# Unnormalised first input products, later S5 parameters and reordered output operands in a two-branch decoder layer

## The chip, the core and the metric

The kernel runs on one core of a Trainium2 chip. Its time is the device time of one execution in microseconds (us); the time before is the median of three runs. A profile records one execution: TensorE's matmuls (PE) and its weight loads (PEld), VectorE (DVE), ScalarE (ACT), GpSimd (POOL), the DMA queues, and SyncE (SP), which issues most of the DMAs. The span of a profile runs from the first to the last recorded instruction.

## What is computed

The reference is one decoder layer with two parallel branches, for 1024 tokens of width 1024 in float32. What matters here is its beginning and its end:

```
h = rms_norm(x, g_pre)                 # x * g_pre / sqrt(mean(x*x) + eps), per token
proj = h @ w_in                        # 512 + 512 + 1280 + 1280 + 1024 + 1024 columns
s5_x, s5_g, lru_x, lru_g, gate_s, gate_l = split(proj)
y_s = s5_ssm(s5_x, ...)                # discretised complex state-space model, 32 groups
z_s = (GLU of gelu(y_s)) * silu(s5_g) @ w_bs
z_l = rg_lru(conv(lru_x)) * silu(lru_g) @ w_bl
merged = sigmoid(gate_s) * z_s + sigmoid(gate_l) * z_l
x = x + rms_norm(merged @ w_out, g_post)
x = x + (p @ w_ple) * sigmoid(x @ w_ple_gate)
```

The factor 1/sqrt(mean(x*x)+eps) belongs to a token, so it can be applied to `h` or to a column of `h @ w_in`; `g_pre` belongs to a row of `w_in`.

## The kernel before

Everything is kept transposed: 128 features on the partitions and 1024 tokens along a row, in two halves of 512. Every large product is split in three: each operand is cut into a rounded part (`hi`, made by ACT) and the rest (`lo = src - hi`, made by DVE or POOL), and `three` (L306 to L310) adds hi*hi, hi*lo and lo*hi in PSUM, so a block of 128x128 weights against 512 tokens is three matmuls. I call twelve such matmuls (two blocks against both halves, or one block pair) a **group**. The weights come in chunks through `Weights`: a DMA from SP, `hi` by ACT (L215), `lo` by DVE (L227), in a ring of six buffers of four blocks; `ahead` prepares a few buffers before TensorE needs them. The instructions of PE, DVE, ACT and POOL stand in the order in which the program writes them, each engine executes its own in that order, and the background generators in `bg` are advanced one step at each `tick`, that is about once a group. So the order of work around the change is fixed by where a step is written or at which tick it is taken.

The stages that the change touches:

- **w_ple.** Eight groups multiply `p` by `w_ple` (m = 0 to 7, tiles `ps_ple`); ACT copies each result to `ple_sb` (L710) and SP stores it. Meanwhile x arrives, ACT squares its eight columns `xt(k)` (L683), DVE adds the squares (L685), and DVE does the first 60 or so small steps of `s5_params`, the parameters of the state-space model (`prep_exp`).
- **The token factor.** `tok_rstd` (L377 on): 16 sums over partitions on PE (`pst_pre`), a short chain on DVE with one square root on ACT, eight diagonal tiles, and eight products that spread the factor over all partitions (`psb_pre`).
- **Two pairs of w_in columns**, u0 with u1 and then u2 with u3 (function `two`, tiles `ps_u`, eight groups each: one group for each column k of x). Before group k of the first pair `h_build` normalises (L729, DVE, the factor read from PSUM), rounds (L730, ACT) and takes the rest (L739, first half DVE, second half POOL). The second pair finds all of `h` ready. ACT takes the results out of PSUM (L748) in the order that the scan needs, and they are stored to DRAM. The rest of `s5_params` stands after the last `h_build` and in the ticks of the second pair; its powers and the input matrix `bb` are made by POOL (L604 to L661).
- **Light rows.** Eighteen products of `h` with one further column of w_in, four groups each (`light`, tiles `ps_L`), each followed by a sigmoid on ACT (L925). In their ticks runs the state-space model (`s5_all`): a table (`s5_table`), output weights on POOL (`s5_out_weights`), and for each of eight head blocks `s5_main`, whose weights `ta` DVE makes from `pw` and `bb` (L827 to L829) and PE transposes (`pwin`, L844).
- **w_out**, late in the kernel, is a block algorithm with sums of operands: `product` is one group, and its operands are B11, B21, T2, T3, T1, B22 and T4, each split in `op_split`. The order of the products is four of B11, two of B21, and then four times T2, T3, T1, B22 (tiles `oY`, `oZ`, `oW`, `oV`); the sums of weights `wS` for them come from POOL (L187) just in time. The operands T1 and B22 are split by the generator `out_ops` in the ticks behind B11.

Of the kernel before, what the change touches and what calls it, by code (L numbers as in the profile page):

```python
# [9 lines left out]
F32 = mybir.dt.float32  # L10
F32R = mybir.dt.float32r
I32 = mybir.dt.int32
AF = mybir.ActivationFunctionType
# [4 lines left out]
P = 128  # L18
# [110 lines left out]
class Weights:  # L129
# [116 lines left out]
def tile_hybrid_trunk(  # L246
# [21 lines left out]
    def page(i, name, dt=F32R):  # L268
        return page_pool[i].tile([P, 2 * NT], dt, tag=f"pg{i}", name=name)
# [36 lines left out]
    def three(ps, wb, xb, start, stop, more=False):  # L306
        (wh, wl), (xh, xl) = wb, xb
        T.matmul(ps, wh, xh, start=start, stop=False, skip_group_check=more)  # L308
        T.matmul(ps, wh, xl, start=False, stop=False, skip_group_check=more)  # L309
        T.matmul(ps, wl, xh, start=False, stop=stop, skip_group_check=more)  # L310
# [14 lines left out]
    def drain():  # L325
        while bg:
            tick()
# [116 lines left out]
    def quarter(t):  # L444
        return t.rearrange("p (k n) -> p k n", n=HT)
# [19 lines left out]
    sqs = [two_rows(i, f"sqs{i}") for i in (0, 1)]  # L465
    ple_sb = [two_rows(i, f"ple_sb{i}") for i in (4, 5, 13, 2)]
    scratch = page(8, "scratch", F32)
    NPAR = sum(n for _, n in SPAR)
    NPT = NPAR - 2048
# [15 lines left out]
    G.memset(toep, 0.0)  # L485
    G.memset(sgn, 1.0)
    G.memset(sgn[64:], -1.0)

    def load_x(ks):
        for k in ks:  # L490
# [170 lines left out]
        G.tensor_tensor(bb_2, bb_2, bt, ALU.add)  # L661

    prep = s5_params()
    seen = []

    def prep_steps(n):
        for _ in range(n):
            next(prep, None)

    def prep_exp(n):  # L670
        for _ in range(n):
            if not seen:
                seen.extend(["exp"] * (next(prep) == "exp"))

    def prep_until(mark):
        while next(prep, mark) != mark:
            pass

    prep_exp(24)

    def square(k):
        sq = sqs[k % 2][:, k // 2 % 2] if k else ssq
        S.activation(sq, xt(k), AF.Square)  # L683
        if 0 < k < ND - 1:
            V.tensor_tensor(ssq, ssq, sq, ALU.add)  # L685
            prep_exp(5)
# [5 lines left out]
    squares = {0: (0,), 1: (1, 2), 2: (3,), 3: (4,), 4: (5, 6), 5: (7,)}  # L692
    for m in range(ND):
        if m % 2 == 0:
            wb = W.next()
        if m == 7:
            prep_exp(100)
            next(stats)
        ps = wide(f"ps_ple{m}")
        for k in range(2):  # L700
            for h in range(2):
                three(ps[:, HALF[h]], wb[2 * (m % 2) + k], (p_hi[:, k, HALF[h]], p_lo[:, k, HALF[h]]), k == 0, k == 1)
        for k in squares.get(m, ()):
            sq = square(k)
            if k == ND - 1:
                ssqs.append(sq)
        if m == 7:
            next(stats)
        sb = ple_sb[m // 2][:, m % 2]
# [6 lines left out]
    for _ in stats:  # L716
        pass

    hq = {n: [quarter(page(i0 + j, f"h{n}{j}")) for j in range(2)]
          for n, i0 in (("B11", 0), ("B21", 4), ("B12", 10), ("B22", 12))}  # L720

    def hplain(k, h):
        hi, lo = hq[f"B{1 + k // 4}{1 + h}"]
        return hi[:, k % 4, :], lo[:, k % 4, :]

    def h_hi(k):
        for h in range(2):
            xs = xt(k, HALF[h])
            V.scalar_tensor_tensor(xs, xs, gpre[:, k:k + 1], rb[h], ALU.mult, ALU.mult)  # L729
            S.activation(hplain(k, h)[0], xs, AF.Copy)  # L730

    def h_build(k):
        if k == 0:
            h_hi(0)
        elif 0 < k < ND - 1:
            h_hi(k + 1)
        for h in range(2):
            hi, lo = hplain(k, h)
            (G if h else V).tensor_tensor(lo, xt(k, HALF[h]), hi.bitcast(F32), ALU.subtract)  # L739
        if k <= 0:  # L740
            h_hi(k + 1)
        if k == ND - 1:
            prep_until("den")

    def u_out(m, ps, tile):
        for h in range(2):
            up = tile(h).rearrange("p (j k) -> p j k", j=8)
            S.activation(up.rearrange("p j k -> p k j"), ps[h].rearrange("p (k j) -> p k j", j=8), AF.Copy)  # L748
# [3 lines left out]
    ups = quarter(page(9, "ups", F32))  # L752
# [3 lines left out]
    for t, ps in enumerate(two(ND, hplain, "u0", h_build, pair_of("u0"))):  # L756
        u_out(t, ps, lambda h: ups[:, 2 * t + h, :])

    def prep_rest():
        for _ in range(2):  # L760
            yield
            prep_steps(2)
        yield
        for _ in prep:
            pass

    bg.append(prep_rest())
    u2, u3 = two(ND, hplain, "u2", ps=pair_of("u2"))
    u_out(2, u2, lambda h: pro.tile([P, HT], F32, tag=f"up{h}", name=f"up{h}"))
    drain()  # L770
    pctx.close()

    ev = s5x.enter_context(tc.tile_pool(name="ev", bufs=2))
# [440 lines left out]
    def x1(k, h):  # L1214
        return x1p[k // 2][:, k % 2, HALF[h]]

    def out_ops():
        for name, i, q in (("T1", 16, 11), ("B22", 7, 22)):
            op(name, i)
            for k in range(4):  # L1220
                op_split(name, k, mg(q, k), k % 2 == 1)
                if k % 2:
                    flush()
                    yield

    def last_op():
        op("T4", 12)
# [35 lines left out]
    def product(ps, name, start):  # L1263
# [3 lines left out]
            three(ps, wb, (hi[:, k, :], lo[:, k, :]), start and k == 0, k == 3, not start)  # L1267
        tick()

    xs = [bank(f"oX{p}") for p in range(4)]  # L1270
    for p_ in range(4):
        product(xs[p_], "B11", True)
        S.activation(mixt(2 * p_, 1), xs[p_], AF.Copy)
        if p_ > 1:
            S.activation(mixt(2 * p_, 0), xs[p_], AF.Copy)
    bg.append(out_ops())
    for p_ in range(2):
        product(xs[p_], "B21", False)
        S.activation(mixt(2 * p_, 0), xs[p_], AF.Copy)
# [164 lines left out]
```

## Time and profile before

| | us |
|---|---|
| median of three runs (lowest, highest) | 977.82 (975.71, 981.02) |
| the profiled execution's own time | 978.07 |
| its span, first to last instruction | 976.3 |
| TensorE busy in the span | 948.3 (97%) |
| VectorE, ScalarE, GpSimd busy | 586.0, 455.7, 160.5 |
| mean granted TensorE clock | 0.995 |

Read the profile by stages and not by its averages: TensorE is busy nearly everywhere, so what counts is each place where it waits, and what that wait ends on. In a row of the timeline stand the start, the duration, the engine, the line of the kernel, the operation, the tile written and the tiles read, the shape and the count, and in square brackets the idle time of that engine before it with its releaser. A matmul's duration overlaps the next one, so the pace of TensorE is read from the distance of two starts.

### The profile page before, as it was taken

The numbers are of one execution on the slowest core, as the hardware profiler recorded it, in microseconds if no ns is written. First come the engines' busy times: TensorE is split into PE (matmuls) and PEld (weight loads), VectorE is DVE, ScalarE is ACT, GpSimd is POOL, SyncE is SP. The second block draws the span as 40 slices with busy tenths as digits, with TensorE's granted clock in tenths as the row PEclk, the third lists the DMA queues.
The fourth block names the chain that finished last, engine by engine and source line by source line (L and its number), as shares of the span: only waits on it lengthen the run. The fifth ranks groups of instructions, "written<-read, shape, count | busy, mean of one in ns | idle before, by whom it ended". The sixth has DMA issues, their size and how long they took to land.

```text
span 976.3 us, 11808 instructions
## 1 busy us (share of the span) xinstructions
PE 948.3 (97%) x4304; PEld 776.9 (80%) x4304; DVE 586.0 (60%) x1017; ACT 455.7 (47%) x654; POOL 160.5 (16%) x177
## 2 busy tenths in 40 slices
PE   7899999999999999999999999999999998999988
PEld 5788777888788888888888888888888876887766
DVE  7853777888761236666666668345311577786832
ACT  7542244334432146666766665233112344458461
POOL 0255421211100000000000000000001345433431
PEclk9999999999999999999999999999999999999999
DMA  9634232333242211111111115742348995399995
GB/s 349 244 80 127 93 101 85 114 115 114 72 118 99 81 49 49 49 49 49 48 49 49 49 40 153 260 151 70 108 135 233 246 194 178 106 244 228 282 267 125
DMA packets 64282, 128.19 MB, mean 131 GB/s; under 512 B 18400, under 2 KB 29024, under 8 KB 64224
## 3 DMA queue, kind: packets, MB, share of 16 engines
q1 hardware_dynamic: 55584, 109.61, 34.4%
q0 software_dynamic: 8640, 17.83, 10.4%
q8 instruction: 34, 0.56, 0.2%
q14 instruction: 24, 0.20, 0.1%
HBM read 84.81 MB, written 27.79 MB: 115 GB/s over the span
## 4 chain that ended last, share of the span: by engine, by line
PE 74%; DVE 11%; issue 6%; DMA 4%; POOL 2%; ACT 1%; SPq 0%; POOLq 0%; DVEq 0%; ACTq 0%
PE ps_L L308 4%; PE ps_L L310 4%; PE ps_L L309 4%; PE ps_rx L308 4%; PE ps_rg L308 4%; PE ps_rg L310 4%; PE ps_rx L310 4%; PE ps_rx L309 4%; PE ps_rg L309 4%; PE ps_bl L310 4%; PE ps_bl L309 4%; PE ps_bl L308 4%; PE ps_pg L310 2%; DMA wq<-wraw 2%; PE ps_pg L309 2%
## 5 line engine op out<-in xcount | busy, mean ns | idle before, releaser
L215 ACT ACTIVATE wq<-wraw 128x512 fp32r<-128x512 f32 (+1 forms) x189 | 112.3, 607 | 96.5 <-PE ps_bl L310 77.3
L219 POOL DMA_DIRECT2D wq<-wraw x52 | 47.9, 920 | 550.6 <-ACT wq L218 527.3
L308 PE MATMUL ps_L<-hB,wq 128*128 128x512 f32 x320 | 127.2, 398 | 0.0
L310 PE MATMUL ps_L<-hB,wq 128*128 128x512 f32 x320 | 124.8, 390 | 0.0
L309 PE MATMUL ps_L<-hB,wq 128*128 128x512 f32 x320 | 124.6, 389 | 0.0
L227 DVE TENSOR_TENSOR wq<-wraw,wq 128x512 fp32r<-128x512 f32 (+1 forms) x137 | 94.5, 707 | 26.5 <-ACT wq L215 26.4
L308 PEld LDWEIGHTS ps_L<-hB,wq 128*128 128x128 f32 x320 | 60.1, 188 | 13.4 <-issue 1.7
L310 PEld LDWEIGHTS ps_L<-hB,wq 128*128 128x128 f32 x320 | 60.1, 188 | 12.9
L309 PEld LDWEIGHTS ps_L<-hB,wq 128*128 128x128 f32 x320 | 60.2, 188 | 11.8
L969 DVE SCALAR_TENSOR_TENSOR c<-ps_rx,cp_t,c 128x1023 f32<-128x1023 f32 (+2 forms) x30 | 38.5, 1282 | 43.6 <-ACT c L967 42.8
L308 PE MATMUL ps_rx<-hB,wq 128*128 128x512 f32 x160 | 62.5, 391 | 0.0
L308 PE MATMUL ps_rg<-hB,wq 128*128 128x512 f32 x160 | 62.5, 391 | 0.0
L310 PE MATMUL ps_rx<-hB,wq 128*128 128x512 f32 x160 | 62.4, 390 | 0.0
L310 PE MATMUL ps_rg<-hB,wq 128*128 128x512 f32 x160 | 62.4, 390 | 0.0
L308 PE MATMUL ps_bl<-yl,wq 128*128 128x512 f32 x160 | 62.3, 389 | 0.0
L310 PE MATMUL ps_bl<-yl,wq 128*128 128x512 f32 x160 | 62.3, 389 | 0.0
L309 PE MATMUL ps_rx<-hB,wq 128*128 128x512 f32 x160 | 62.2, 389 | 0.0
L309 PE MATMUL ps_rg<-hB,wq 128*128 128x512 f32 x160 | 62.2, 389 | 0.0
L309 PE MATMUL ps_bl<-yl,wq 128*128 128x512 f32 x160 | 62.2, 389 | 0.0
L1080 DVE TENSOR_TENSOR blg<-blg,ps_bl 128x1024 f32<-128x1024 f32 x8 | 9.8, 1222 | 68.7 <-PE ps_bl L310 68.6
L925 ACT ACTIVATE sg<-ps_L 128x1024 f32<-128x1024 f32 x20 | 20.5, 1027 | 61.9 <-PE ps_L L310 45.5
L310 PE MATMUL ps_pg<-x1hl,wq 128*128 128x512 f32 x120 | 47.3, 394 | 2.0 <-DMA wq<-wraw 2.0
(345 smaller groups left out, 2183.0 us busy)
## 6 DMA issues: line engine op xcount, KB each, us to landing
wraw<-w_blocks SPq DMA_DIRECT2D x90, 512.0 KB, 4.0
wq<-wraw POOLq DMA_DIRECT2D x52, 256.0 KB, 6.3
xt<-x_t SPq DMA_DIRECT2D x8, 512.0 KB, 7.3
ple_d<-ple_sb SPq DMA_DIRECT2D x8, 512.0 KB, 8.5
sgl_d<-sg SPq DMA_DIRECT2D x8, 512.0 KB, 4.9
sgs_d<-sg SPq DMA_DIRECT2D x8, 512.0 KB, 3.9
blg<-sgl_d SPq DMA_DIRECT2D x8, 512.0 KB, 4.6
ms_d<-blg SPq DMA_DIRECT2D x8, 512.0 KB, 2.9
```

Of the source, the lines that this page charges most:

```text
L215: nc.scalar.activation(hi, src, AF.Copy)
L219: nc.gpsimd.dma_start(lo.bitcast(F32), src, accum_op=ALU.add)
L227: self.nc.vector.tensor_tensor(lo, src, hi.bitcast(F32), ALU.subtract)
L308: T.matmul(ps, wh, xh, start=start, stop=False, skip_group_check=more)
L309: T.matmul(ps, wh, xl, start=False, stop=False, skip_group_check=more)
L310: T.matmul(ps, wl, xh, start=False, stop=stop, skip_group_check=more)
L925: S.activation(t, ps, AF.Sigmoid)
L969: V.scalar_tensor_tensor(c[:, d:], ps[:, :NT - d], w_[3 - d], c[:, d:], ALU.mult, ALU.add)
L1080: V.tensor_tensor(gs[d], gs[d], t, ALU.mult)
```

## The change

1. **The first pair multiplies x*g_pre without the token factor.** New `raw(k)` makes the two parts of `x*g_pre` (ACT with a scale, DVE one three-operand step over 1024 tokens), six of them between the w_ple groups and two at the start of the pair. The token factor's steps stand between the groups of the first pair. Its value is copied from PSUM to `rbs` in SBUF, and DVE multiplies it into the results as they leave PSUM (`u_out(..., scaled=True)`).
2. **The normalised `h`**, which the second pair and all later rows use, is made by `normed(k)`: columns 0 and 1 in the last two groups of the first pair, the others one group each, two groups ahead, in the second pair. DVE now reads x and `rbs` from SBUF, over 1024 tokens.
3. **The squares of columns 1, 3 and 5 go to POOL**; `ple_sb` has four buffers in place of eight, and pages are handed out anew.
4. **All of `s5_params` is moved into the ticks of the light rows**, ten of its steps at a tick, ahead of the table of the state-space model (`prep_all`). The steps themselves are the same. They issue no DMA.
5. **Ten small matmuls** on a constant stand at the start.
6. **In w_out, T1 has a generator of its own** that starts ahead of the B11 products; B22 starts where T1 started.

```
+    for _ in range(10):
+        T.matmul(warm[:, :P], ones, ones, start=True, stop=True)
...
+    def prep_all(n):
+        for i, _ in enumerate(prep):
+            if i % n == n - 1:
+                yield
...
+    def raw(k):
+        hi, lo = hpage(k, "xg")
+        S.activation(hi, xt(k), AF.Identity, scale=gpre[:, k:k + 1])
+        V.scalar_tensor_tensor(lo, xt(k), gpre[:, k:k + 1], hi.bitcast(F32), ALU.mult, ALU.subtract)
...
+        if k in (1, 3, 5):
+            G.tensor_tensor(sq, xt(k), xt(k), ALU.mult)
+        else:
+            S.activation(sq, xt(k), AF.Square)
...
+    raws = {0: 0, 1: 1, 2: 2, 3: 3, 5: 4, 6: 5}
...
+    def normed(k):
+        hi, lo = hpage(k, "h")
+        V.scalar_tensor_tensor(xt(k), xt(k), gpre[:, k:k + 1], rbs, ALU.mult, ALU.mult)
+        S.activation(hi, xt(k), AF.Copy)
         for h in range(2):
...
+            (G if h else V).tensor_tensor(
+                lo[:, HALF[h]], xt(k, HALF[h]), hi[:, HALF[h]].bitcast(F32), ALU.subtract)
+
+    def before_u0(k):
+        if k < 2:
+            raw(6 + k)
+        if k > 1:
+            next(stats, None)
+        if len(rb) == 2 and k < 6:
+            for h in range(2):
+                S.activation(rbs[:, HALF[h]], rb[h], AF.Copy)
+        if k > 5:
+            normed(k - 6)
+
+    def before_u2(k):
+        if k + 2 < ND:
+            normed(k + 2)
...
+            if scaled:
+                V.tensor_tensor(dst, src, rbs[:, HALF[h]].rearrange("p (k j) -> p k j", j=8), ALU.mult)
+            else:
+                S.activation(dst, src, AF.Copy)
...
     def s5_all():
+        yield from prep_all(10)
         yield from s5_table(0)
...
-    def out_ops():
-        for name, i, q in (("T1", 16, 11), ("B22", 7, 22)):
...
+    def t1_ops():
+        op("T1", 16)
+        for k in range(4):
+            if k == 3:
+                yield
+                yield
+            op_split("T1", k, mg(11, k), k % 2 == 1)
+            if k:
+                flush()
+                yield
+
+    def b22_ops():
+        op("B22", 7)
+        for k in range(4):
+            op_split("B22", k, mg(22, k), k % 2 == 1)
+            if k % 2:
+                flush()
+                yield
...
+    bg.append(t1_ops())
     xs = [bank(f"oX{p}") for p in range(4)]
...
-    bg.append(out_ops())
+    bg.append(b22_ops())
```

**VectorE through the second pair of w_in columns.** In these rows of the kernel before, which stand in the first pair, `xt` is a column half of x, `psb_pre` the token factor in PSUM, `hB` the split of `h`:

```order
L729 SCALAR_TENSOR_TENSOR xt_107<-xt_107,cp_t,psb_pre_422 128x512
L729 SCALAR_TENSOR_TENSOR xt_107<-xt_107,cp_t,psb_pre_433 128x512
L739 TENSOR_TENSOR hB_443<-xt_107,hB_442 128x512
L729 SCALAR_TENSOR_TENSOR xt_108<-xt_108,cp_t,psb_pre_422 128x512
L729 SCALAR_TENSOR_TENSOR xt_108<-xt_108,cp_t,psb_pre_433 128x512
L739 TENSOR_TENSOR hB_443<-xt_107,hB_442 128x512
```

In the changed kernel the same work stands in the second pair, behind the four scaled results of the first (`ups`); `sdp` holds the token factor in SBUF, `h` is the split:

```order
L754 TENSOR_TENSOR ups<-ps_u_363,sdp 128x64x8 x2
L754 TENSOR_TENSOR ups<-ps_u_364,sdp 128x64x8 x2
L728 SCALAR_TENSOR_TENSOR xt_107<-xt_107,cp_t,sdp 128x1024
L731 TENSOR_TENSOR h_548<-xt_107,h_548 128x512
L227 TENSOR_TENSOR wq_468<-wraw_275,wq_468 128x512
L227 TENSOR_TENSOR wq_553<-wraw_373,wq_553 128x512
L728 SCALAR_TENSOR_TENSOR xt_107<-xt_107,cp_t,sdp 128x1024
L731 TENSOR_TENSOR h_573<-xt_107,h_573 128x512
```

Before, a column was normalised ahead of the `lo` step of the column before it; now each column's `lo` step follows its own normalising step at once, with ACT's rounding between the two.

**ScalarE around the first light row.** Before, the sigmoid of the first row (`sg` from `ps_L`) was followed by weights and by the copy of the first transposed S5 weights (`win` from `pwin`):

```order
L925 ACT_TABLE_LOAD
L925 ACTIVATE sg_910<-ps_L_816 128x1024
L215 ACTIVATE wq_914<-wraw_677 128x512
L846 ACTIVATE win_966<-pwin_961 128x512
L215 ACTIVATE wq_968<-wraw_677 128x512
```

Now the two sine steps of the S5 parameters (tile `scratch`) stand behind that sigmoid:

```order
L925 ACT_TABLE_LOAD
L925 ACTIVATE sg_832<-ps_L_706 128x1024
L215 ACTIVATE wq_836<-wraw_559 128x512
L600 ACT_TABLE_LOAD
L600 ACTIVATE scratch<-scratch 128x160
L601 ACTIVATE scratch<-scratch,halfpi 128x160
L215 ACTIVATE wq_950<-wraw_559 128x512
L925 ACT_TABLE_LOAD
L925 ACTIVATE sg_985<-ps_L_835 128x1024
```

The sine steps were in the first w_in pair before, ahead of every sigmoid. On TensorE the first `pwin` stood six groups behind the start of the light rows, and now stands eleven groups behind it, that is seven groups behind the end of the first row.

**ScalarE in w_out.** Before, around the two B21 products, T1 (`mT_5958`) was rounded first and B22 (`mB_6014`) came behind the weights `wq_5996`, which are made of a sum from POOL (`wS_151`):

```order
L215 ACTIVATE wq_5967<-wS_147_5876 128x512
L1150 ACTIVATE mT_5958<-mg_5530 128x512
L1279 ACTIVATE mix_5964<-oX_5840 128x512
L1255 ACTIVATE sq<-oX_5840 128x512
L215 ACTIVATE wq_5996<-wS_151_5973 128x512
L1150 ACTIVATE mB_6014<-mg_5531 128x512
L215 ACTIVATE wq_6022<-wraw_5872 128x512
L1150 ACTIVATE mB_6014<-mg_5532 128x512
```

Now B22 (`mB_5987`) stands where T1 stood, ahead of the corresponding weights, which are `wq_6025` here:

```order
L1150 ACTIVATE mB_5987<-mg_5550 128x512
L1290 ACTIVATE mix_5993<-oX_5858 128x512
L1262 ACTIVATE ssq<-oX_5858 128x512
L215 ACTIVATE wq_5996<-wS_147_5902 128x512
L1150 ACTIVATE mB_5987<-mg_5551 128x512
L1290 ACTIVATE mix_5993<-oX_5859 128x512
L1265 ACTIVATE sq<-oX_5859 128x512
L215 ACTIVATE wq_6025<-wS_151_6002 128x512
```

T1's four roundings moved up among the B11 products.

More of the change, by code (lines that the diff above doesn't have):

```diff
@@ L464, in tile_hybrid_trunk @@
     pf, p_hi, p_lo = two_rows(12, "pf"), two_rows(3, "p_hi", F32R), two_rows(6, "p_lo", F32R)
-    sqs = [two_rows(i, f"sqs{i}") for i in (0, 1)]
-    ple_sb = [two_rows(i, f"ple_sb{i}") for i in (4, 5, 13, 2)]
+    sqs = [two_rows(i, f"sqs{i}") for i in (1, 5)]
+    ple_sb = [two_rows(i, f"ple_sb{i}") for i in (2, 13)]
     scratch = page(8, "scratch", F32)
@@ L663, in tile_hybrid_trunk, with hplain, hpage @@
     prep = s5_params()
[L664 to L679, printed above, removed]
+    def prep_all(n):
+        for i, _ in enumerate(prep):
+            if i % n == n - 1:
+                yield
+    hp = (10, 11, 0, 4, 12, 1, 5, 13)
+    hx = {}
+    def hplain(k, h):
+        return hx[k][:, 0, HALF[h]], hx[k][:, 1, HALF[h]]
+    def hpage(k, name):
+        hx[k] = page(hp[k], f"{name}{k}").rearrange("p (s n) -> p s n", s=2)
+        return hx[k][:, 0], hx[k][:, 1]
+    def raw(k):
+        hi, lo = hpage(k, "xg")
+        S.activation(hi, xt(k), AF.Identity, scale=gpre[:, k:k + 1])
+        V.scalar_tensor_tensor(lo, xt(k), gpre[:, k:k + 1], hi.bitcast(F32), ALU.mult, ALU.subtract)
     def square(k):
         sq = sqs[k % 2][:, k // 2 % 2] if k else ssq
-        S.activation(sq, xt(k), AF.Square)
+        if k in (1, 3, 5):
+            G.tensor_tensor(sq, xt(k), xt(k), ALU.mult)
+        else:
+            S.activation(sq, xt(k), AF.Square)
         if 0 < k < ND - 1:
             V.tensor_tensor(ssq, ssq, sq, ALU.add)
-            prep_exp(5)
         return sq
@@ L702, in tile_hybrid_trunk @@
                 three(ps[:, HALF[h]], wb[2 * (m % 2) + k], (p_hi[:, k, HALF[h]], p_lo[:, k, HALF[h]]), k == 0, k == 1)
+        if m in raws:
+            raw(raws[m])
         for k in squares.get(m, ()):
@@ L706, in tile_hybrid_trunk @@
                 ssqs.append(sq)
-        if m == 7:
-            next(stats)
-        sb = ple_sb[m // 2][:, m % 2]
+        sb = ple_sb[m // 2 % 2][:, m % 2]
         S.activation(sb, ps, AF.Copy)
@@ L715, in tile_hybrid_trunk @@
             W.fetch(11)
[L716 to L726, printed above, removed]
-        for h in range(2):
-            xs = xt(k, HALF[h])
-            V.scalar_tensor_tensor(xs, xs, gpre[:, k:k + 1], rb[h], ALU.mult, ALU.mult)
-            S.activation(hplain(k, h)[0], xs, AF.Copy)
@@ L732, in h_build @@
[L732 to L745, printed above, removed]
+    rbs = ssq
+    def normed(k):
+        hi, lo = hpage(k, "h")
+        V.scalar_tensor_tensor(xt(k), xt(k), gpre[:, k:k + 1], rbs, ALU.mult, ALU.mult)
+        S.activation(hi, xt(k), AF.Copy)
+        for h in range(2):
+            (G if h else V).tensor_tensor(
+                lo[:, HALF[h]], xt(k, HALF[h]), hi[:, HALF[h]].bitcast(F32), ALU.subtract)
@@ L749, in u_out @@
             nc.sync.dma_start(
                 u_d[m].rearrange("g c j k -> (g c) j k")[:, :, 64 * h:64 * h + 64], up)
-    ups = quarter(page(9, "ups", F32))
+    ups = quarter(page(3, "ups", F32))
     def pair_of(name):
         return [[t[:, HALF[h]] for h in range(2)] for t in (wide(f"ps_{name}{i}") for i in range(2))]
[L756 to L765, printed above, removed]
@@ L767, in tile_hybrid_trunk @@
-    bg.append(prep_rest())
-    u2, u3 = two(ND, hplain, "u2", ps=pair_of("u2"))
+    for t, ps in enumerate(two(ND, hplain, "u0", before_u0, pair_of("u0"))):
+        u_out(t, ps, lambda h: ups[:, 2 * t + h, :], scaled=True)
+    u2, u3 = two(ND, hplain, "u2", before_u2, pair_of("u2"))
     u_out(2, u2, lambda h: pro.tile([P, HT], F32, tag=f"up{h}", name=f"up{h}"))
-    drain()
     pctx.close()
```

15 lines of the change are left out of this document (4 added, 11 removed).

## The prediction

> **What bounds the kernel now.** The page says where the time is, the waits of TensorE and four windows say where it is lost.
>
> ```profile
> span 976.3 us, 11808 instructions
> PE 948.3 (97%) x4304; PEld 776.9 (80%) x4304; DVE 586.0 (60%) x1017; ACT 455.7 (47%) x654; POOL 160.5 (16%) x177
> ...
> PE oV L309 <- DVE mB L1157: 2.4, 2, 2.2
> ...
> PE oV L308 <- ACT mB L1150: 1.7, 1, 1.7
> ...
> 0.00:25.00 25.00, 17.97 (x64) 1.00 0.93 350
> 25.00:50.00 25.00, 21.52 (x109) 0.93 0.60 228
> 400.00:425.00 25.00, 25.00 (x111) 1.00 0.18 50
> 800.00:825.00 25.00, 20.95 (x87) 0.97 0.58 182
> ```
>
> A full window holds 111 matmuls. The two places with fewer, the first 50 us and w_out at 800 to 825 us, are the ones the change works on; between them TensorE is nearly saturated, so whatever newly holds it there is paid in full. The first stage runs in the kernel before like this:
>
> ```profile
> 11.46 0.39 PE L308 MATMUL ps_ple<-p_hi,wq 128*128 128x512 f32 x1
> ...
> 38.58 0.49 PE L308 MATMUL ps_u<-hB,wq 128*128 128x512 f32 x1 [0.67 <-ACT hB L730]
> ...
> 45.18 0.80 PE L309 MATMUL ps_u<-hB,wq 128*128 128x512 f32 x1 [2.01 <-DVE hB L739]
> 45.77 0.63 PE L310 MATMUL ps_u<-hB,wq 128*128 128x512 f32 x1
> 46.20 0.63 PE L308 MATMUL ps_u<-hB,wq 128*128 128x512 f32 x1
> ...
> 48.70 0.40 PE L308 MATMUL ps_u<-hB,wq 128*128 128x512 f32 x1
> 48.93 0.39 PE L309 MATMUL ps_u<-hB,wq 128*128 128x512 f32 x1
> ...
> 87.47 0.39 PE L308 MATMUL ps_L<-hB,wq 128*128 128x512 f32 x1
> ```
>
> Two starts lie 0.23 us apart at full clock (48.70, 48.93; 0.227 over long runs), and 0.43 in the eight matmuls behind the 2.01 us gap: an idle TensorE costs the gap and then about 8 x 0.2 = 1.6 us. A group of twelve is 2.72 us, the eight groups of a pair are 21.8.
>
> **The start, until the light rows (before: 87.47 us).** The token factor no longer stands between w_ple and the first pair, its work on TensorE stays:
>
> ```profile
> 29.76 3.46 PE pst_pre L380 x32
> 36.12 1.80 PE psb_pre L400 x16
> ```
>
> If nothing waited, seven groups behind 11.46 (1.2 earlier, if the ten matmuls raise the clock) would end w_ple at 29.3. But VectorE now has five `raw` steps, six sums and four weight parts ahead of the first pair's second half block, and GpSimd has three squares. The nearest rows:
>
> ```profile
> 10.57 1.06 ACT L683 ACTIVATE sdp<-xt 128x1024 f32<-128x1024 f32 x1 [0.54 <-DMA xt<-x_t]
> ...
> L685 DVE TENSOR_TENSOR sdp<-sdp,sqs 128x1024 f32<-128x1024 f32 x6 | 7.3, 1221 | 0.1
> L999 DVE SCALAR_TENSOR_TENSOR ta<-sq,ta 128x1024 f32<-128x1024 f32 x10 | 12.2, 1219 | 2.1 <-ACT sq L997 2.1
> L739 DVE TENSOR_TENSOR hB<-xt,hB 128x512 fp32r<-128x512 f32 x8 | 5.6, 706 | 0.0
> ...
> 41.36 1.30 POOL L739 TENSOR_TENSOR hB<-xt,hB 128x512 fp32r<-128x512 f32 x1 [0.57 <-ACT hB L730]
> 41.83 1.38 DVE L227 TENSOR_TENSOR wq<-wraw,wq 128x512 fp32r<-128x512 f32 x1 [1.22 <-ACT wq L215]
> ```
>
> The last two rows show VectorE and GpSimd taking turns: a step that takes 0.7 alone took 1.38, since it began 0.47 into GpSimd's 1.30. So I add both: 11 x 1.22 + 4 x 0.7 + three squares of 2 x 1.3 = 24.0 us. x arrives for ACT's first step at 10.57; behind that step, of 1.1, the sum can begin at 11.7, so the weights are there at 35.7, where TensorE wants them at 29.3 + 1.4. I take 35.0, since part of the first square runs while VectorE still waits. The first pair ends at 35.0 - 1.4 + 21.8 + 3.5 + 1.8, plus 1.0 for the VectorE chain of the factor, which two groups do not quite cover: 61.7, against 87.47 - 21.8 = 65.7 before.
>
> The Trainium skill says why the turns occur (SBUF — State Buffer, Who interferes with whom): a VectorE instruction with two SBUF inputs and a GpSimd instruction that reads SBUF exclude each other for a whole instruction. The rows above agree. By that page `normed`, whose factor now lies in SBUF and no longer in PSUM, has become such an instruction.
>
> The second pair had no wait (eight groups from 65.7 to 87.47); now it is fed by a chain, per column: VectorE 1.22, ACT, VectorE 0.7, and only then the next column.
>
> ```profile
> L748 ACT ACTIVATE ups<-ps_u 128x512 f32<-128x512 f32 x4 | 3.9, 1136 | 0.1
> ```
>
> That is 1.22 + 1.06 + 0.7 = 3.0 us, with a GpSimd half in the way up to 4.3, where a group takes 2.72; I take 3.4, nearer to the free chain since GpSimd gets a turn only when VectorE waits. Column 2 starts 3.1 us after the pair begins (four scaled results of 1.13, the row of ACT's, begun 1.4 early). With six columns (20.4), four weight parts (2.8) and the last eight matmuls (1.8) the pair ends 28.1 us after 61.7, at 89.8: **+2.3 us**. Ends: no turns at all, 57.4 + 25.6 = 83.0, that is -4.5; all turns lost, 61.7 + 33.5 = 95.2, that is +7.7. The ten matmuls I cost at nothing: VectorE's 24 us hide them; without that cover they give the 1.2. The halved `ple_sb` too: the page's row below has a store landed after 8.5 us, and its buffer is wanted again four groups, 10.9 us, later; each us above that would hold ACT, and the pair behind it, by as much.
>
> ```profile
> ple_d<-ple_sb SPq DMA_DIRECT2D x8, 512.0 KB, 8.5
> ```
>
> **The light rows.** The moved parameters issue some 90 small VectorE steps, two sines with two more table loads on ACT, and 54 GpSimd steps, no DMA. ACT executes in order, so the sines wait until TensorE has ended the first light row. I follow the chain from there.
>
> ```profile
> 98.35 0.39 PE L308 MATMUL ps_L<-hB,wq 128*128 128x512 f32 x1
> 98.55 1.03 ACT L925 ACTIVATE sg<-ps_L 128x1024 f32<-128x1024 f32 x1 [6.17 <-PE ps_L L310]
> 99.47 0.62 ACT L215 ACTIVATE wq<-wraw 128x512 fp32r<-128x512 f32 x1
> ...
> 58.99 1.28 ACT L596 ACT_TABLE_LOAD   x1
> 63.77 0.34 ACT L596 ACTIVATE scratch<-scratch 128x160 f32<-128x160 f32 x1 [3.49 <-DVE scratch L595]
> 64.01 0.41 ACT L597 ACTIVATE scratch<-scratch,halfpi 128x160 f32<-128x160 f32 x1
> 64.46 0.33 DVE L599 SCALAR_TENSOR_TENSOR sinp<-scratch 128x160 f32<-128x160 f32 x1 [0.72 <-ACT scratch L597]
> 65.38 0.63 POOL L606 TENSOR_TENSOR pw<-scratch,cosp 128x32 f32<-128x32 f32 x1 [4.53 <-DVE cosp L601]
> 84.15 1.30 POOL L661 TENSOR_TENSOR bb<-bb,braw 128x512 f32<-128x512 f32 x1
> L828 DVE TENSOR_TENSOR tb<-pw,bb 128x512 f32<-128x512 f32 x8 | 9.3, 1168 | 0.0
> L829 DVE TENSOR_TENSOR ta<-ta,tb 128x512 f32<-128x512 f32 x8 | 6.6, 824 | 0.3
> ```
>
> ACT: 0.2 + 0.9 + 0.6 + 1.3 + 0.7 = 3.7 us to the end of the second sine; VectorE 64.46 to 65.38, 0.95 with the gap; GpSimd from 65.38 to 85.45, 20.1 us without a pause; then 1.2 + 0.8 = 2.0 for the weights `ta` that `pwin` transposes. Sum 26.7 us. TensorE reaches `pwin` seven groups after that row, 7 x 2.72 = 19.1 us, and stands: 7.6 us, and the clock's 1.6 behind it: **+9.2 us**. Before, GpSimd was done at 85.45, ahead of all light rows. Ends: VectorE's turns have drawn out some of GpSimd's steps; I allow 1.8 us for that, an estimate of five steps like the first shown (0.63) at some 0.35 each. The last two steps can double by turns, as at 41.83, to 4.0. So 5.8 to 9.6 us of stall, 7.4 to 11.2 with the clock.
>
> Behind VectorE's wait for GpSimd (the reciprocal, half-way) are queued the table and the weights of the fourth row: due eight groups, 21.8 us, behind the first row, free after 3.7 + 1.0 + 9.4 + 2.5. They cost nothing.
>
> **w_out.** B22 came late because its rounding stood on ACT behind weights that GpSimd had not summed:
>
> ```profile
> 815.85 0.40 PE L310 MATMUL oW<-mT,wq 128*128 128x512 f32 x1
> 816.70 0.63 ACT L215 ACTIVATE wq<-wS 128x512 fp32r<-128x512 f32 x1 [5.40 <-POOL wS L187]
> 817.24 0.61 ACT L1150 ACTIVATE mB<-mg 128x512 fp32r<-128x512 f32 x1
> 828.03 0.40 PE L308 MATMUL oZ<-mT,wq 128*128 128x512 f32 x1
> ```
>
> From the first row to the last, 25 starts at 0.227 would take 5.7 us and took 12.2: 6.5 us lost, 4 of them in the two waits and the rest at the lower clock. Moved up, B22 has no such weight ahead of it and the waits go. Next late: T1's extra steps delay B21's fourth part and the weights of the next T2, by at most 1.3 us as I order the steps. **-5.2 us**, between -6.5 and -3.0.
>
> The skill's window (TensorE: Matmul & The Clock Gate, What's actually happening) lowers the clock after about 3.4 us idle; by it these waits, at most 1.7 and 2.2 us, would not, and the saving would be some 1.6 us smaller. The rows at 45.77 show the low pace after 2.01, so the trace decides.
>
> **Sum**, on the profiled execution's 978.07 us (0.25 above the median of the runs): 2.3 + 9.2 - 5.2 = +6.3, that is **984.4 us**.
>
> **Rivals.**
> - *VectorE and GpSimd hardly hinder each other* (for it: the eight L739 steps took 706 ns in the mean, with GpSimd at work beside them; against: 1.38 at 41.83): start -4.5, total 977.6, no change.
> - *The first transpose is not held* (the other side). It is one mechanism, the chain sine, GpSimd, `ta` in front of `pwin`: below 19.1 us it costs nothing. Against: GpSimd alone shows 20.1. Without it 2.3 - 5.2 = -2.9, 975.2; with the better start 968.4.
> - *VectorE starves the second pair* with all turns lost: start +7.7, total 989.8. For it: both inputs in SBUF. Against: that mean of 706.
>
> **Chances.** Forecast 0.44, own range 979 to 990; of the rivals 0.24, 0.18 and 0.14. About 0.5% (4.9 us) is what a measurement of this kernel can tell from no change, so the borders are 973.2 and 983.0. Slower: 0.33 of the forecast and the third rival's 0.14, 0.47. Same: 0.10, 0.18 and 0.10, 0.38. Faster, the rest: 0.15. The range leaves out the ends of the second and third rival: 973.0 to 991.5.
>
> **What would show it.** In the changed profile `ps_L` starts at about 90 us, waits of `ps_u` on `h` are new in the second pair, `pwin` shows one wait on `ta` of 6 to 9 us and starts 0.43 us apart behind it, and the waits of `oV` on `mB` are gone. A light stage with no wait at the first `pwin`, or a second pair without waits, would make it wrong.

## The result, and the profile after

The changed kernel takes 993.89 us (median of 6 runs, 992.28 to 994.24); the kernel before took 979.21 beside it (975.71 to 982.34). The ratio is 1.015, with a 95% interval of 1.0123 to 1.0177: 12 to 17 us slower. The forecast, 984.4 us, had the sign right and less than half the size, and its range ended below, at 991.5.

First the page of after, span and busy time, and then the waits of TensorE (in all, times, longest).

```profile
span 992.0 us, 11868 instructions
PE 955.9 (96%) x4324; PEld 780.4 (79%) x4324; DVE 615.0 (62%) x1021; ACT 457.7 (46%) x650; POOL 168.9 (17%) x180
```

```profile
PE pwin L843 <- DVE ta L828: 15.6, 5, 14.3
PE ps_u L308 <- ACT h L729: 2.7, 2, 1.4
PE oX L309 <- DVE mB L1157: 1.7, 1, 1.7
...
PE ps_u L308 <- ACT ple_sb L717: 1.2, 1, 1.2
...
PE ps_u L309 <- DVE h L731: 1.1, 5, 0.2
PE ps_u L309 <- POOL h L731: 1.1, 6, 0.2
```

One wait of 14.3 us at the first transpose is most of it; the second pair now waits for `h` in many small pieces; the waits of `oV` on `mB` are gone. Cut at the first matmul of each stage, the two profiled executions differ like this (us):

| stage | before | after | difference | forecast |
|---|---|---|---|---|
| until the second pair | 65.7 | 62.5 | -3.2 | -4.0 |
| second pair | 21.8 | 32.5 | +10.7 | +6.3 |
| light rows | 237.0 | 250.9 | +13.9 | +9.2 |
| between, until w_out (`oX`) | 467.0 | 467.0 | 0 | 0 |
| w_out, until `ps_pg` | 85.0 | 81.1 | -3.9 | -5.2 |
| last stage | 99.9 | 98.1 | -1.8 | 0 |

The last row is no part of the change: in twelve other kernels of this study, all with the same last stage, it takes 97.3 to 98.5 us, so it was the 99.9 of before that was long. The start scatters too: two kernels with the same start reached the light rows at 87.5 and 90.9 us.

The second pair, one column of it, from the timelines of VectorE, GpSimd, ACT and TensorE of after. Its first matmul stands at the head, the first of the light rows at the end.

```profile
62.46 0.39 PE L308 MATMUL ps_u<-h,wq 128*128 128x512 f32 x1
...
77.62 0.69 DVE L731 TENSOR_TENSOR h<-xt,h 128x512 fp32r<-128x512 f32 x1 [1.12 <-ACT h L729]
77.67 1.78 POOL L731 TENSOR_TENSOR h<-xt,h 128x512 fp32r<-128x512 f32 x1 [2.25 <-ACT h L729]
78.23 2.31 DVE L728 SCALAR_TENSOR_TENSOR xt<-xt,cp_t,sdp 128x1024 f32<-128x1024 f32 x1
80.57 1.06 ACT L729 ACTIVATE h<-xt 128x1024 fp32r<-128x1024 f32 x1 [2.98 <-DVE xt L728]
81.66 0.69 DVE L731 TENSOR_TENSOR h<-xt,h 128x512 fp32r<-128x512 f32 x1 [1.13 <-ACT h L729]
...
94.97 0.39 PE L308 MATMUL ps_L<-h,wq 128*128 128x512 f32 x1
```

Both halves of a remainder become ready at once. VectorE takes its half first (0.69), GpSimd's half runs behind it until 79.45, and only then does VectorE's normalising step of the next column run: 2.31 us, where alone it takes 1.28. Then VectorE waits 1.13 for ACT. A column takes 81.66 - 77.62 = 4.04 us, a group of TensorE 2.72. This holds for the columns without weights in between; where two weight parts stand ahead of the normalising step, they lose the turn in its place (2.38 us for both, 1.29 alone), and the column takes 5.3 to 5.4.

The light rows, the chain to the first transpose, from the timelines of after:

```profile
106.06 1.03 ACT L925 ACTIVATE sg<-ps_L 128x1024 f32<-128x1024 f32 x1 [6.16 <-PE ps_L L310]
...
109.60 0.33 DVE L603 SCALAR_TENSOR_TENSOR sinp<-scratch 128x160 f32<-128x160 f32 x1 [2.15 <-ACT scratch L601]
...
110.52 0.25 POOL L610 TENSOR_TENSOR pw<-scratch,cosp 128x32 f32<-128x32 f32 x1 [17.44 <-DVE cosp L605]
...
119.10 0.35 DVE L636 RECIPROCAL scratch<-scratch 128x32 f32<-128x32 f32 x1 [8.65 <-POOL scratch L634]
...
128.07 1.39 POOL L665 TENSOR_TENSOR bb<-bb,braw 128x512 f32<-128x512 f32 x1
...
135.19 1.55 DVE L797 TENSOR_TENSOR tt<-tt,sb 128x128 f32<-128x128 f32 x1
...
136.66 1.00 DVE L826 TENSOR_TENSOR ta<-pw,bb 128x512 f32<-128x512 f32 x1
...
139.37 1.12 PE L843 MATMUL pwin<-ident,ta 128*128 128x128 f32 x4 [14.31 <-DVE ta L828]
```

GpSimd is done at 129.5, 19 us after its start, about as forecast. But VectorE begins `ta` at 136.66: from the reciprocal on it works at the table of the state-space model (L786 to L797), 17.3 us with two weight parts in it. Beside it GpSimd makes the input matrix and, from 129.4 on, the output weights that stand behind it. The kernel before took 5.8 for the same table and one weight part, with GpSimd idle beside it.

In w_out, the first matmul and the new wait:

```profile
812.82 0.48 PE L308 MATMUL oX<-mB,wq 128*128 128x512 f32 x1 [1.41 <-DVE mg L1206]
...
827.89 0.50 PE L309 MATMUL oX<-mB,wq 128*128 128x512 f32 x1 [1.66 <-DVE mB L1157]
```

### The profile page after: what moved, and what is told of

It reads as the page before. It is cut to its first block, busy times and chain, and to the rows that moved or that the text cites. A ratio compares the mean times of both kernels' runs of the same rounds, so it can differ in the third digit from the quotient of the medians.

```text
span 992.0 us, 11868 instructions
## 1 busy us (share of the span) xinstructions
PE 955.9 (96%) x4324; PEld 780.4 (79%) x4324; DVE 615.0 (62%) x1021; ACT 457.7 (46%) x650; POOL 168.9 (17%) x180
## 4 chain that ended last, share of the span: by engine, by line
PE 70%; DVE 14%; issue 7%; ACT 3%; POOL 3%; DMA 3%; SPq 1%; POOLq 0%; DVEq 0%; ACTq 0%
PE ps_L L308 5%; PE ps_L L309 5%; PE ps_L L310 5%; PE ps_rg L308 4%; PE ps_rx L308 4%; PE ps_rx L310 4%; PE ps_rg L310 4%; PE ps_rx L309 4%; PE ps_rg L309 4%; PE ps_bl L310 4%; PE ps_bl L309 4%; PE ps_bl L308 4%; DVE wq L227 2%; PE ps_pg L310 2%; PE ps_pg L309 2%
## 5 line engine op out<-in xcount | busy, mean ns | idle before, releaser
L308 PE MATMUL ps_L<-h,wq 128*128 128x512 f32 x320 | 127.8, 399 | 0.0
L309 PE MATMUL ps_L<-h,wq 128*128 128x512 f32 x320 | 125.1, 391 | 0.0
L310 PE MATMUL ps_L<-h,wq 128*128 128x512 f32 x320 | 125.1, 391 | 0.0
L227 DVE TENSOR_TENSOR wq<-wraw,wq 128x512 fp32r<-128x512 f32 (+1 forms) x137 | 96.8, 725 | 4.7 <-ACT wq L215 4.6
L308 PEld LDWEIGHTS ps_L<-h,wq 128*128 128x128 f32 x320 | 60.4, 189 | 13.5 <-issue 1.7
L310 PEld LDWEIGHTS ps_L<-h,wq 128*128 128x128 f32 x320 | 60.4, 189 | 12.9
L309 PEld LDWEIGHTS ps_L<-h,wq 128*128 128x128 f32 x320 | 60.5, 189 | 11.8
L308 PE MATMUL ps_rx<-h,wq 128*128 128x512 f32 x160 | 62.5, 391 | 0.0
L308 PE MATMUL ps_rg<-h,wq 128*128 128x512 f32 x160 | 62.5, 391 | 0.0
L310 PE MATMUL ps_rx<-h,wq 128*128 128x512 f32 x160 | 62.4, 390 | 0.0
L310 PE MATMUL ps_rg<-h,wq 128*128 128x512 f32 x160 | 62.4, 390 | 0.0
L309 PE MATMUL ps_rx<-h,wq 128*128 128x512 f32 x160 | 62.3, 389 | 0.0
L309 PE MATMUL ps_rg<-h,wq 128*128 128x512 f32 x160 | 62.3, 389 | 0.0
L310 PE MATMUL ps_pg<-x1hl,wq 128*128 128x512 f32 x120 | 47.4, 395 | 1.0 <-DMA wq<-wraw 1.0
L309 PE MATMUL ps_pg<-x1hl,wq 128*128 128x512 f32 x120 | 47.3, 394 | 0.8 <-DVE x1hl L1157 0.8
```

The lines of the kernel that those rows point to most:

```text
L227: self.nc.vector.tensor_tensor(lo, src, hi.bitcast(F32), ALU.subtract)
```

## Experiments

My theory after this reading: the loss is two separate things, the place of the S5 parameters (+14 in the light rows) and the order of steps that feeds the second pair (+11); both are delays of TensorE by VectorE.

### The single parts on the kernel before

**The w_out part alone.** Only `t1_ops` and `b22_ops` in place of `out_ops`.

> The kernel before with only the w_out part of the change (T1 split ahead of B22). The traces of before and after put this part at -3.9 us, first product of w_out to first product of the stage behind it (84.96 us before, 81.08 after), and show the stage behind it 1.8 us shorter. If both belong to this edit, the run comes out 5.7 us below before; if the shorter last stage has another cause, 3.9 below; by the forecast 5.2. If the gain needs the late start that the rest of the change gives w_out, it is under 2.

Ratio 0.9959 (0.9945 to 0.9974), -4.0 us: the edit's own worth, independent of the rest. w_out takes 80.3 us there (85.0 before), and one new wait remains:

```profile
PE oX L309 <- DVE mB L1157: 1.0, 1, 1.0
```

**The ten matmuls alone.**

> The kernel before with only the ten small matmuls at the start. Forecast: up to 1.2 us less where nothing hides it. In the trace of after the low pace behind the first wait is still there (8 matmuls at 0.43 from 9.35 on), so I expect no difference, 0 to -0.5 us. The rival, that they do raise the clock, gives -1.2 and no low pace in the first 15 us.

Ratio 1.002 (1.0003 to 1.0037): no gain, but 2 us more, 0.3 to 3.6. Where they come from stays open; its profile shows the light rows 1.8 us longer, with a wait of 1.3 at the first transpose. The low pace behind the first waits, which after still has, is gone in this run, against what I expected: of the ten kernels with the ten matmuls only after has it, and all four without them have it. So they do raise the pace there; the pair of kernels at the end shows where the gain goes.

**The parameters alone**, on the start of the kernel before:

```
-    bg.append(prep_rest())
...
     def s5_all():
+        yield from prep_all(10)
         yield from s5_table(0)
```

> The kernel before with only the S5 parameters moved into the ticks of the light rows; the second pair stays as it was and leaves VectorE free. Theory now: the stall at the first transpose is GpSimd's chain (19 us behind the sines) plus the state-space table, which stands between them on VectorE and takes turns with GpSimd; both are there without the rest of the change, so the stall is 12 to 15 us and the run 11 to 15 us above before. The forecast's chain, without the table: stall 7.6, +9.2. Rival: the parameters are late only because the second pair now keeps VectorE busy until 93 us; then the stall is under 4 us here and the run at most 4 above before.

Ratio 1.0107 (1.007 to 1.0143), +10.5 us; the light rows are 14.2 us longer than before (251.2 against 237.0). The run lost less than that stage: in the profiles two stages that this edit leaves alone are shorter than before, w_out by 2.3 us and the last stage by 2.6, for which I have no cause.

```profile
132.56 1.11 PE L819 MATMUL pwin<-ident,ta 128*128 128x128 f32 x4 [14.32 <-DVE ta L804]
```

The stall is the same to 0.01 us, though VectorE is free from 79 us on in this second pair and has done all steps ahead of the sines by 98.6. The sines still wait for the first sigmoid, at 99.24, as the forecast had it. So the busy second pair is not the cause; the rival falls.

### The stall at the first transpose

**`ta` ahead of the table**, on after:

```
         V.tensor_tensor(wt, wt, wu, ALU.subtract)
+        if hb == 0:
+            yield from first        # the table
+            s5_out_weights(0)
```

> The kernel after, with one thing moved: the three VectorE steps that make the first transposed weights stand ahead of the table of the state-space model and not behind it, and the first output weights on GpSimd behind them. Theory: the last parameter is there at 129.5 us, the steps take 2.7, so the first transpose starts at about 132.2 and not at 139.4, and the run is 7 us below after; some of it is lost (up to 2) if the weights queued behind become late. Rival: the table is hidden and the stall is GpSimd's chain alone: the same time as after, or within 1 us of it.

Ratio to before 1.0132 (1.01 to 1.0164), where after has 1.015: 1.8 us less, within the uncertainty, and not the 5 to 7 that I expected. So the reading goes by the profile. The timeline of TensorE at the first and the second transpose:

```profile
134.28 1.11 PE L846 MATMUL pwin<-ident,ta 128*128 128x128 f32 x4 [7.61 <-DVE tt L787]
...
162.71 0.63 PE L846 MATMUL pwin<-ident,ta 128*128 128x128 f32 x4 [3.34 <-DVE ta L826]
```

The `tt` named in the first row is a memset right behind `ta`, whose last step ended at 134.22. The first stall goes from 14.31 to 7.61 us: 6.7 us were the table, beside which GpSimd's output weights were moved too. What is left is the chain of sines, GpSimd and `ta`, as long as the forecast's 7.6, in part by luck: GpSimd takes 18.7 us where the forecast had 20.1, and `ta`, once its last operand is there, 3.4 where it had 2.0, since its steps now take turns with the output weights. Half comes back at the second head block, whose weights queue behind the table; the light rows are 247.4 us long, 3.5 less.

### The second pair

Four kernels from after; the light rows, and their 14 us, are left as they are. "Pair" is the second pair's time.

| kernel | us a column | pair | ratio to before (95%) |
|---|---|---|---|
| after | 4.04 | 32.5 | 1.015 (1.0123 to 1.0177) |
| GpSimd's half on VectorE | 3.62 | 29.9 | 1.0129 (1.0095 to 1.0163) |
| factor from PSUM | 3.14 | 30.7 | 1.0125 (1.0091 to 1.0158) |
| next column's step first | 2.87 | 23.5 | 1.0062 (1.0044 to 1.0079) |
| both of the last two | - | 21.8 | 1.0039 (1.002 to 1.0059) |

**GpSimd's half on VectorE**: `(G if h else V)` becomes `V` in `normed`.

> The kernel after, with the second half of each remainder of h made by VectorE and not by GpSimd, so that VectorE does 0.6 us more a column and GpSimd nothing in the second pair. In the trace of after the second pair takes 32.5 us and a column 4.04: the normalising step 2.31, of which 1.1 are spent behind GpSimd's half, ACT 1.1, VectorE's half 0.6. Theory (VectorE and GpSimd take turns for whole steps): without GpSimd a column takes 1.2 + 1.2 + 1.2 = 3.6, the weight parts shrink from 2.4 to 1.3 as well, the second pair takes 28 to 29 us and the run is about 4 below after. Rival (the turns are free, VectorE's own chain is the limit): a column takes 0.6 more, the pair 36, the run 3.6 above after.

```profile
75.89 1.28 DVE L728 SCALAR_TENSOR_TENSOR xt<-xt,cp_t,sdp 128x1024 f32<-128x1024 f32 x1
78.29 1.29 DVE L731 TENSOR_TENSOR h<-xt,h 128x512 fp32r<-128x512 f32 x2 [1.12 <-ACT h L729]
79.51 1.28 DVE L728 SCALAR_TENSOR_TENSOR xt<-xt,cp_t,sdp 128x1024 f32<-128x1024 f32 x1
```

More work for VectorE, and a column is 0.4 us shorter: the normalising step takes 1.28 in place of 2.31. The turns are real. The rival, a longer pair, falls.

**The factor from PSUM**: two halves with `rb[h]` in place of one step with `rbs`.

> The kernel after, with the factor for the normalised h read from PSUM in two halves of 512, as the kernel before reads it, and not from the copy in SBUF; GpSimd keeps its half. Theory: it is the second SBUF operand that makes the normalising step wait for GpSimd; with PSUM the step takes 1.4 (two halves of 0.7) and begins at once, a column 3.2 us in place of 4.04, the second pair about 27 us in place of 32.5, and the run is 4 to 6 below after. Rival: the step waits for GpSimd wherever its factor lies; the same time as after, or 1 above.

VectorE and GpSimd in this kernel:

```profile
75.85 0.69 DVE L733 TENSOR_TENSOR h<-xt,h 128x512 fp32r<-128x512 f32 x1 [1.13 <-ACT h L731]
75.90 1.80 POOL L733 TENSOR_TENSOR h<-xt,h 128x512 fp32r<-128x512 f32 x1 [1.34 <-ACT h L731]
76.46 1.40 DVE L730 SCALAR_TENSOR_TENSOR xt<-xt,cp_t,psb_pre 128x512 f32<-128x512 f32 x2
78.99 0.69 DVE L733 TENSOR_TENSOR h<-xt,h 128x512 fp32r<-128x512 f32 x1 [1.13 <-ACT h L731]
```

With its second operand in PSUM the step runs at once beside GpSimd's half, 1.40 for both halves; a column is 3.14, the 3.2 I expected. The pair gained less than that, 30.7 and not 27, since the weight parts still take turns (2.38 for two) and the last matmuls of the pair started 0.43 apart, which cost some 1.4. As the Trainium skill has it (SBUF — State Buffer, Who interferes with whom), two SBUF inputs exclude a GpSimd step that reads SBUF; these rows agree. The runs of these two kernels, 2 us below after by their ratios, are within the uncertainty; their columns are not.

**The next column's step first:**

```
     def normed(k):
-        V.scalar_tensor_tensor(xt(k), ...)
+        if k + 1 < ND:
+            product(k + 1)      # the same step, one column ahead
```

> The kernel after, with the normalising step of column k+1 written ahead of the two halves of the remainder of column k, so that VectorE works while ACT rounds; factor from SBUF, GpSimd keeps its half. Theory (turns): what can't overlap is VectorE's 1.2 + 0.6 and the weights' 0.65 and GpSimd's 1.1 to 1.3 a column, 3.5 to 3.8 us in place of 4.04, so the second pair is only 2 to 4 us shorter than 32.5. Rival (the loss is the order, VectorE idle while ACT rounds): TensorE's own 2.72 a column decide, the pair takes 23 to 24 us, the run is 8 to 9 below after.

The rival was right: the pair takes 23.5 us and the run is 8.6 below after (1.0062 against 1.015). The timelines of VectorE and TensorE:

```profile
62.35 0.39 PE L308 MATMUL ps_u<-h,wq 128*128 128x512 f32 x1
...
74.41 2.31 DVE L727 SCALAR_TENSOR_TENSOR xt<-xt,cp_t,sdp 128x1024 f32<-128x1024 f32 x1
76.64 0.68 DVE L737 TENSOR_TENSOR h<-xt,h 128x512 fp32r<-128x512 f32 x1
77.24 1.27 DVE L727 SCALAR_TENSOR_TENSOR xt<-xt,cp_t,sdp 128x1024 f32<-128x1024 f32 x1
78.44 1.78 DVE L737 TENSOR_TENSOR h<-xt,h 128x512 fp32r<-128x512 f32 x1
...
85.83 0.39 PE L308 MATMUL ps_L<-h,wq 128*128 128x512 f32 x1
```

The turns are still there (2.31, 1.78), but VectorE no longer waits for ACT, and two columns take 5.74 us. My 3.5 to 3.8 a column had charged the weight parts to every column and forgot the columns that are ready ahead.

**Both:**

> The kernel after with both edits, the factor from PSUM and the next column's normalising step first. Nothing of the step is held then, VectorE's own work is 1.4 + 0.6 + 0.65 = 2.65 us a column beside TensorE's 2.72: the second pair takes 22 to 24 us, the run is 8 to 10 below after. If the turns of the remaining steps (VectorE's half and the weights against GpSimd's half) still matter, 25 to 27 us and 5 to 7 below.

No wait is left in the second pair, 21.8 us, TensorE's own time, and the run is 1.0039 of before. The one loss that remains against before is the light rows' 14 us; in the profiles the start (-2.0), w_out (-4.8) and the last stage (-1.7) are shorter than in before.

### A version that is faster than both

**The parameters ahead of the light rows again**, on the kernel with both edits: a few of VectorE's small steps behind the first weights, more behind the first raw product, the rest ahead of `raw(6)`, the sines at the sixth group of the first pair, GpSimd's pieces one at a time behind `normed`.

> The kernel after with the factor from PSUM and the next column's step first (983.4 us), and the S5 parameters back ahead of the light rows, spread over the pauses of the start: VectorE's small steps at 10 to 15 us, 36 to 44 and 52 to 56, the sines behind the token factor, GpSimd's powers one piece at a time in the second pair, only the input matrix in the light rows. Theory: the light rows' +14 us come from the place of the parameters alone, so nearly all of it goes: 969 to 973 us, 1% below before; GpSimd's pieces may hold the second half of some remainders, up to 3 us of it given back. Rival (the start has no room for them, TensorE waits there for what it no longer waits for in the light rows): 976 to 983.

970.75 us, ratio 0.993 (0.9907 to 0.9954), faster than both kernels. The first transpose waits no longer: the light rows take 235.2 us. The second pair gives back 2.7 (24.5 against 21.8), as I had allowed: one remainder waits 1.3 us behind GpSimd's powers. That the parameters' place makes the 14 us is shown from both sides.

```profile
PE ps_ple L310 <- DVE wq L227: 4.0, 1, 4.0
...
PE pwin L872 <- DVE ta L857: 1.1, 3, 0.4
```

**The same without the ten matmuls:**

> The same kernel without the ten small matmuls at the start. Alone on the kernel before they made it 2 us slower (0.3 to 3.6). If that is their own cost, this run is 1 to 3 us below the one with them; if it was the start's scatter from run to run (the light rows began at 87.5 and 90.9 us in two runs with the same start), both are equal within 1.5 us; if the matmuls do raise the clock here, this run is up to 1.2 above.

970.56 us and 0.993 again. One matmul of w_ple from each timeline, first of the kernel without the ten:

```profile
9.06 0.77 PE L309 MATMUL ps_ple<-p_lo,wq 128*128 128x512 f32 x1
9.62 0.63 PE L310 MATMUL ps_ple<-p_hi,wq 128*128 128x512 f32 x1
...
23.11 0.50 PE L310 MATMUL ps_ple<-p_hi,wq 128*128 128x512 f32 x1 [2.80 <-DVE wq L227]
```

```profile
9.12 0.40 PE L308 MATMUL ps_ple<-p_hi,wq 128*128 128x512 f32 x1
9.36 0.40 PE L309 MATMUL ps_ple<-p_lo,wq 128*128 128x512 f32 x1
...
23.34 0.50 PE L310 MATMUL ps_ple<-p_hi,wq 128*128 128x512 f32 x1 [4.04 <-DVE wq L227]
```

With the ten matmuls TensorE is at full pace here (0.24 us between starts, 0.43 to 0.56 without), and then waits 4.04 in place of 2.80 us for the same weights: the 1.2 us are gained and lost again. The forecast's cover, VectorE's queue, is right for these two kernels; in the profile of after itself that queue held TensorE for 0.67 us only, and the low pace was still there.

**The weights ahead of raw products and squares**, and then **all squares on ACT**:

> The kernel with the parameters early (970.75 us), with the weights made ahead of each group's raw products and squares and not behind them, and its eight small VectorE steps behind the first raw product moved to the first pair. There TensorE waits 4.0 us at 23 us for the third weight part, which stands on VectorE behind two raw products, a sum and GpSimd's squares. Theory: that queue sets when the first pair begins (the forecast's first step); with the weights first the wait is gone and the run is 2 to 4 us below, 967 to 969. Rival: the wait only moves (to the stored results of w_ple, 1.2 us in after, or to the token factor), and the run is within 1.5 us of the one before it.

> The same kernel with all eight squares on ACT, as in the kernel before the change. The forecast has the three squares on GpSimd cost VectorE 2.6 us each by turns. Theory: the sums then wait for no GpSimd step and VectorE's queue is up to 5 us shorter, while ACT has 3 us more: up to 2 us below the run with the squares on GpSimd where VectorE's queue still sets the start. Rival: ACT, whose copies free TensorE's banks of w_ple, becomes the late one: 1 to 3 us above it.

Ratios 0.9929 (0.9903 to 0.9955) and 0.9923 (0.9894 to 0.9952): neither differs from the kernel they start from. The waits of TensorE and the copies of ACT in the first of them:

```profile
PE ps_u L308 <- ACT ple_sb L731: 3.3, 2, 2.5
...
PE ps_ple L310 <- DVE wq L227: 1.0, 1, 1.0
```

```profile
26.56 1.03 ACT L731 ACTIVATE ple_sb<-ps_ple 128x1024 f32<-128x1024 f32 x1 [3.83 <-DMA ple_d<-ple_sb]
```

The rival was right: the wait for weights shrinks from 4.0 to 1.0, and another takes its place, ACT's copy of a w_ple result that waits for the store of an earlier one, since `ple_sb` has two buffer pairs and no longer four (that four would remove it was not tried). With all squares on ACT the weights are on time and the wait of 3.2 for `ple_sb` stays; what the squares' place is worth can't be told from no difference.

## Why the prediction was too small

The forecast had +6.3 us and the two profiles differ by 15.7. Of the 9.4 between them 4.7 are in the light rows, 4.4 in the second pair, 1.3 in w_out and 0.8 in what stands ahead of the second pair; the last stage gives 1.8 back. By the runs, -4.0 for w_out and +10.5 for the parameters, measured alone, leave some 8 us of the 14.7 for the rewritten start (to about 5 either way, by the intervals), and the stage table has +7.5.

- **The first pair came out near the forecast** (end 61.7, 62.5 in the trace), but by luck, since the pieces differ: w_ple ended 1.5 us earlier than I let VectorE's queue hold it, and the factor's chain, priced at 1.0, held nothing; a wait of 1.2 for `ple_sb` and a low pace of 1.7 took that back. The halved `ple_sb`, which I "cost at nothing", was wrong by that 1.2: ACT waited 3.07 us for a store. The first copy ended at 13.83, but SyncE issued its store, behind fetches of weights, only at 16.59, and ACT could go on 9.4 us after that.
- **The failed step in the second pair** is the price of a column: "I take 3.4, nearer to the free chain since GpSimd gets a turn only when VectorE waits". It takes 4.04. VectorE's and GpSimd's halves wait for the same rounding, so GpSimd's turn falls behind VectorE's half in each column, right before the step that the chain needs, or before the weight parts ahead of it. From the third column's remainder to the eighth's (68.27 to 91.13) five columns and four weight parts take 22.9 us where the forecast's prices give 19.8: 3.1 of the 4.4 that the pair is longer than forecast. The other 1.3 are at the end: the last eight matmuls wait for GpSimd's half of the last column, which is there at 92.97, and I had them wait for VectorE's alone. That is the third rival, "all turns lost", which had the light rows at 95.2; they begin at 94.97. Its mechanism is the one that the rows show, but that its number fits so well is luck: it began the pair 0.8 us too early and had it 1.0 too long. The mean of 706 that I held against it was that of VectorE's halves, which begin first; the step behind them had its factor in PSUM and took no turn. And even my 3.0 had a larger part: VectorE's idle wait for ACT, which the order of the steps made and one edit removed (-8.6 us).
- **The failed step in the light rows** is what I put at nothing, "Behind VectorE's wait for GpSimd are queued the table and the weights of the fourth row ... They cost nothing". I checked only the weights' due time there. `ta` itself stands behind the table, and the table behind the reciprocal. At its old 5.8 us the table would have been hidden by GpSimd's remaining ten; beside GpSimd's steps it took 17.3. That the turns with GpSimd draw it out is read from the rows; for the table it was not tried by itself. The other links were right as links, and their sum too, by luck: without the table the stall is 7.61, forecast 7.6, with two errors of 1.4 that cancel. The light rows are 4.7 longer than forecast and not 6.7, mostly since the waits for the input that is read back from DRAM (`pin` on `U`) sum to 2.4 us in before and 0.8 in after.
- **w_out** was right in kind, -4.0 alone. All of the 6.5 us that were lost there are gone, the low pace too; but the new wait of B21's fourth part and a short one for the weights of the next T2 lose 2.4 with their restarts, where I had allowed up to 1.3.
- **The ten matmuls** bring nothing in the runs: alone they came out 2 us slower, and in the pair of kernels with and without them the next wait takes back what they gain.
- The rivals "hardly hinder each other" and "the first transpose is not held" are refuted.

## What to carry to other kernels

When a step is moved behind a wait, follow the queue of that engine from the wait to the next step that the critical engine needs, and count everything that stands between, at the pace it has beside its new neighbours. A chain over three engines (VectorE, ACT, VectorE) that feeds TensorE wants the next item's first step ahead of the last step of this item; here that was worth 8.6 us, more than the place of the operands. A gain at the start is kept only if the next resource, here the store buffers, has slack.

## What the runs showed of the hardware

For their length, small VectorE steps beside a busy GpSimd lose far more than large ones. The later ones of the table's steps, 0.2 to 0.4 us each in the kernel before, took up to 1.6 beside GpSimd's of 1.0 to 1.7; the durations of the 28 steps add up to 16.8 us in place of 5.9. The large normalising step went from 1.28 to 2.31.

TensorE's pace can fall without a gap. In after the 32 one-column sums `pst_pre` run without a pause, and soon behind them full matmuls start 0.43 apart:

```profile
42.29 0.36 PE L380 MATMUL pst_pre<-ones,sqs 128*128 128x1 f32 x2
...
43.72 0.63 PE L309 MATMUL ps_u<-xg,wq 128*128 128x512 f32 x1
44.15 0.63 PE L310 MATMUL ps_u<-xg,wq 128*128 128x512 f32 x1
```

Of the ten kernels with these sums inside the first pair, eight show it, with 6 to 13 slow matmuls, up to 2.6 us; two show none. Nor does a wait of given length always bring the low pace: behind one of 2.24 us in the kernel with the next column's step first seven starts lie 0.43 apart, behind one of 2.80 in the kernel with the parameters early and without the ten matmuls none does. So the prediction's 1.6 us behind an idle TensorE is not a constant. The Trainium skill (TensorE: Matmul & The Clock Gate, What's actually happening) speaks of an idle window of about 3.4 us that runs freely; 3.5 us of one-column products seem to count as idle here, and a window that runs freely would fit the varying number. That they count so was not tried by itself.
